# Attention in groups of four query blocks, with the rotary queries of all heads made in the gate-projection stage

## The chip, the cores and the metric

The kernel runs on one core of one Trainium2 chip. The metric is the device time of one execution in microseconds (us), median of three runs. The engines are named as in the profile: PE (TensorE) multiplies matrices, with PEld its weight loads; DVE (VectorE), ACT (ScalarE) and POOL (GpSimd) compute; SP (SyncE) issues most DMAs. L661 is line 661 of the kernel before.

## What is computed

One layer of a streaming encoder, 1024 tokens of width 1024, all in float32: multi-head latent attention with 16 heads, then a gated per-layer embedding. Cut to what matters here:

```python
u = h @ w_in                                  # h = rmsnorm(x)
c_q, c_kv, k_rope, z = split(u)               # 384, 256, 32, 1024 wide
q = rmsnorm(c_q) @ w_q_b                      # 16 heads x (64 + 32 rotary)
kv = rmsnorm(c_kv) @ w_kv_b                   # 16 heads x (64 key + 64 value)
for blk in range(8):                          # blocks of 128 queries
    s = (q_nope . k_nope + q_rope . k_rope) * scale      # keys up to the block's end
    s = where(k_chunk <= q_chunk, s, -inf)               # chunks of 64
    o = softmax(s) @ v
x = x + (o * silu(z)) @ w_out
x = x + sigmoid(rmsnorm(x) @ ple_gate) * (p @ ple_proj)
out = rmsnorm(x, final_norm)
```

Query block i of a head needs the keys of blocks 0 to i, so its scores are 128 x (i+1)*128.

## The kernel before

To hold float32 precision, every operand of a product is split into a high and a low part (`hi`, `lo`, of type fp32r), and a product is the three matmuls hi*hi, hi*lo and lo*hi. Only the product of probabilities with values differs: there the high and low parts of v lie side by side in the 128 columns of one weight tile, and each key block takes two matmuls, one with the high part of the probabilities (`pt..h`) and one with the low part (`pt..l`).

The stages, in order of time:

- **u** (up to 69 us): `u_tile` (L203 to L232) projects eight tiles of 128 tokens to c_q, c_kv and k_rope; `rsqrt` (L93) is three Newton steps on DVE, begun with a shift and a subtraction on the float's bits.
- **z** (69 to 161 us): the loop over c at L503 makes eight blocks of the gate, 48 matmuls of 512 columns each (L513), evicted by DVE (L516) and put through SiLU by ACT. `z_weights` (L347) loads and splits the weights as it goes (L360 on ACT, L361 on DVE). Beside it run `rope_key` (after block 1), `rope_tables` (after block 2: cosine and sine tables by way of DRAM, L446 on DVE, L452 and L485 as DMAs issued by POOL), `weights(0)` (after block 3) and `project_r(0, ...)` (after blocks 4 and 5).
- **attention** (161 to 507 us): 128 blocks (16 heads, 8 query blocks each) in the order `ORDER`. For block n the loop at L685 issues `scores` (L598: matmuls L609, mask L612 and maximum L614 on DVE, exponential L619 on ACT), then work that prepares the next heads, then `prob_transposes` of block n-2 (L641: transposes L121 on PE, high part L650 on ACT, low part L91 on DVE), then `values` for a pair of query blocks that was finished at block n-4 (L653: matmuls L661, addition of the two halves L664 on ACT and L665 on DVE, product with the gate L667 on POOL, on DVE in the last two heads).
- **out, gate and end** (507 us to the end): eight tiles of the output projection, then eight of the gate of the embedding (both L751), the last norm, and the stores to DRAM (L845). `out_part` (L676) prepares the first operand inside the attention's end, and `normalise` (L622) divides by the sums, by way of a small DRAM tile.

What prepares the next heads: `project_k`, `project_q` and `project_v` (L546, L586, L564), and `project_r(g, hf)` (L427), the rotary part of the queries of four heads. It runs 9 matmuls (L423), two DVE multiplications by cosine and sine (L435), a copy on ACT (L438), a subtraction on POOL (L439, recorded as L91) and two DMAs to DRAM on POOL (L441). Group 0 is made during z, groups 1 to 3 in the heads with h%4 == 2 at the block positions `R_AT`. `rope_q(h)` (L578) loads a head's part from DRAM by SP. All of them go through one pair of tiles, `rt` and `rh`.

The tile framework puts each engine's instructions in an order of its own, by priority (the order of the program) and by when it expects them to be ready; at run time each engine then keeps its order and waits on semaphores. PSUM has eight banks of 512 columns: two tiles `big` of two banks each, and four single banks, tag `one`, shared by the transposes, the values and the projections. A block with more than 128 keys has its scores in `big`:

```python
spans = {128: [(0, 256)], 640: [(0, 384), (384, 640)]}.get(
    n, [(a, min(a + 512, n)) for a in range(0, n, 512)])
ps = ps_big() if n > P else ps_tr()
```

The transposed probabilities of a pair of query blocks stand side by side, 256 columns for each key block; where the first block of a pair has no such key block, a block of zeros stands (L539). So the values of pair g are 2(g+1) key blocks times two matmuls of 256 columns.

## Time and profile before

| | us |
|---|---|
| median of 3 runs | 718.59 (717.83 to 719.44) |
| the profiled execution, whole | 719.65 |
| its span in the profile | 717.9 |
| PE busy | 703.2 (98%) |
| DVE, ACT, POOL busy | 523.8, 400.5, 214.2 |
| granted TensorE clock | 0.998 of full speed |

The profile is of one execution. Times in it count from the span's start. A PE matmul is recorded with its passage through the array, so that records overlap: what a matmul costs in a dense row is the distance of the starts, not the recorded length. The chain of waits lists, for a run of instructions without a gap, their number and the time they took together, and from this the cost of one is read.

### The profile page before, as it was taken

To read this page: it belongs to the slowest core of one execution; us is meant where nothing else is said; L and a number is where in the kernel's file an instruction comes from. 1 tells how busy PE (TensorE), PEld (TensorE's weight loads), DVE (VectorE), ACT (ScalarE), POOL (GpSimd) and SP (SyncE) were. 2 spreads that over 40 slices of the span, in tenths; PEclk is the share of its full clock that TensorE was granted. 3 is DMA by queue.
4 is the path that set the end of the run, shared out by engine and by line. 5 is a ranking of instruction groups with operands and counts; after the bars stand their busy time and mean duration, and the time that the engine had idled before them with its cause. 6 is when DMAs were issued, how large, how long until landed. Compare 5 with 4: busy or idle time off the path is not lost.

```text
span 717.9 us, 11582 instructions
## 1 busy us (share of the span) xinstructions
PE 703.2 (98%) x4032; PEld 612.9 (85%) x4032; DVE 523.8 (73%) x1298; ACT 400.5 (56%) x920; POOL 214.2 (30%) x236
## 2 busy tenths in 40 slices
PE   9999999999999999999999999989999999999995
PEld 7999888888988899889988899878878888888884
DVE  6995553417888888888888888899564168888754
ACT  6752343417777767877767787776353145342322
POOL 0000443214145434554335532264155142000000
PEclk9999999999999999999999999999999999999999
DMA  8720334314103402052211421032573030111101
GB/s 318 279 89 12 122 100 125 103 60 110 38 16 108 147 31 74 1 181 74 66 40 60 136 60 60 15 108 85 179 265 115 1 102 24 38 37 37 60 30 59
DMA packets 26907, 63.95 MB, mean 89 GB/s; under 512 B 4568, under 2 KB 8544, under 8 KB 26848
## 3 DMA queue, kind: packets, MB, share of 16 engines
q1 hardware_dynamic: 23168, 52.19, 22.8%
q0 software_dynamic: 3536, 11.02, 4.6%
q8 instruction: 32, 0.52, 0.3%
q14 instruction: 27, 0.22, 0.1%
q10 hardware_dynamic: 144, 0.00, 0.0%
HBM read 50.01 MB, written 13.18 MB: 88 GB/s over the span
## 4 chain that ended last, share of the span: by engine, by line
PE 90%; DVE 3%; ACT 3%; DMA 2%; issue 1%; POOL 0%; SPq 0%; ACTq 0%; DVEq 0%
PE ps_big L751 21%; PE ps_big L609 13%; PE ps_big L513 12%; PE ps_o L661 10%; PE ps_tr L121 9%; PE ps_pj L423 6%; PE ps_big L215 4%; PE ps_pj L751 3%; PE ps_pj L570 3%; PE ps_pj L553 3%; PE ps_big L216 3%; PE ps_o L215 1%; PE ps_pj L216 1%; DMA wst<-in_w_out 1%; ACT prob L619 1%; PE ps_tr L609 1%
## 5 line engine op out<-in xcount | busy, mean ns | idle before, releaser
L751 PE MATMUL ps_big<-w,aTh 128*128 128x512 f32 (+1 forms) x480 | 139.0, 390 | 0.0
L751 PEld LDWEIGHTS ps_big<-w,aTh 128*128 128x128 f32 x480 | 89.4, 188 | 20.2
L619 ACT ACTIVATE prob<-ps_big,mx 128x384 f32<-128x384 f32 (+6 forms) x112 | 89.4, 798 | 16.2 <-DVE mx L614 15.5
L614 DVE TENSOR_REDUCE mx<-ps_big 128x1 f32<-128x384 f32 (+6 forms) x112 | 91.6, 818 | 1.8
L121 PE MATMUL ps_tr<-ident,prob 128*128 128x128 f32 x576 | 84.1, 273 | 2.0 <-ACT prob L619 2.0
L751 PE MATMUL ps_big<-w,aTl 128*128 128x512 f32 (+1 forms) x240 | 84.6, 390 | 0.0
L121 PEld LDWEIGHTS ps_tr<-ident,prob 128*128 128x128 f32 x576 | 68.3, 140 | 11.7 <-ACT prob L619 2.8
L91 DVE TENSOR_TENSOR pt8l<-ps_tr,pt8h 128x512 fp32r<-128x512 f32 (+3 forms) x128 | 71.0, 582 | 4.5 <-ACT pt8h L650 3.8
L667 POOL TENSOR_TENSOR zT<-o,zT 64x256 f32<-64x256 f32 x56 | 41.1, 736 | 94.2 <-DVE o L665 80.6
L609 PE MATMUL ps_big<-k_hi,qh 128*128 128x512 f32 (+2 forms) x176 | 67.7, 385 | 0.9 <-ACT prob L619 0.8
L650 ACT CAST pt8h<-ps_tr 128x512 fp32r<-128x512 f32 (+3 forms) x128 | 60.7, 509 | 4.7 <-PE ps_tr L121 4.3
L609 PE MATMUL ps_big<-k_lo,qh 128*128 128x512 f32 (+2 forms) x176 | 62.0, 352 | 0.0
L609 PE MATMUL ps_big<-k_hi,ql 128*128 128x512 f32 (+2 forms) x176 | 61.4, 349 | 0.0
L661 PE MATMUL ps_o<-pt8h,vals 128*128 128x256 f32 x224 | 57.6, 294 | 0.0
L661 PE MATMUL ps_o<-pt8l,vals 128*128 128x256 f32 x224 | 55.0, 282 | 0.0
L751 PEld LDWEIGHTS ps_big<-w,aTl 128*128 128x128 f32 x240 | 45.0, 188 | 10.2 <-POOL aTl L91 0.5
L116 ACT ACTIVATE jk<-xs 128x512 bf16<-128x512 f32 (+2 forms) x25 | 18.8, 751 | 45.2 <-DVE xs L829 37.3
L661 PEld LDWEIGHTS ps_o<-pt8l,vals 128*128 128x128 f32 x224 | 42.9, 191 | 0.0
L661 PEld LDWEIGHTS ps_o<-pt8h,vals 128*128 128x128 f32 x224 | 42.6, 190 | 0.0
L650 ACT CAST pt4h<-ps_tr 128x384 fp32r<-128x384 f32 (+3 forms) x64 | 27.2, 426 | 27.3 <-PE ps_tr L121 27.1
L360 ACT ACTIVATE zh<-zs,g_col 128x128 fp32r<-128x128 f32 x56 | 18.3, 392 | 42.1 <-DMA zs<-in_w_z 36.1
L609 PEld LDWEIGHTS ps_big<-k_hi,qh 128*128 128x128 f32 x176 | 33.2, 189 | 7.7 <-ACT prob L619 3.5
(285 smaller groups left out, 1740.2 us busy)
## 6 DMA issues: line engine op xcount, KB each, us to landing
...
```

The lines of the kernel that those rows point to most:

```text
L91: eng.tensor_tensor(out=lo, in0=src, in1=hi.bitcast(F32), op=ALU.subtract)
L121: nc.tensor.transpose(dst[:, j * P:(j + 1) * P], src[:, j * P:(j + 1) * P], ident)
L215: nc.tensor.matmul(pq, st, mv[:, k, :QL], start=first, stop=last)
L423: nc.tensor.matmul(ps, w[b][:, k, :], (cq_hi, cq_lo)[a][:, k, hf * 512:hf * 512 + 512], start=k == 0 and a + b == 0, stop=k == n - 1 and a ...
L513: nc.tensor.matmul(ps[:, hf * 512:(hf + 1) * 512], wz[b][:, k % 4, :], (hT_hi, hT_lo)[a][:, k, hf * 512:(hf + 1) * 512], start=k == 0 and ...
L609: nc.tensor.matmul(ps[:, off + s0:off + s1], q[a][:, qs], (k_hi, k_lo)[b][e][:, s0:s1], start=a + b == 0, stop=a == 1)
L614: V.tensor_reduce(out=mx, in_=s, axis=AX.X, op=ALU.max, negate=True)
L619: A.activation(out=pr[:, :n], in_=s, func=AF.Exp, bias=mx, scale=1.0, accum_out=l)
L650: A.copy(out=hi[:, j0:j0 + n, half], in_=src)
L661: nc.tensor.matmul(ps[:, :256], w, z[:, j, :], start=j + n == 0, stop=j == last and n == 1)
L667: (V if h >= H - 2 else G).tensor_tensor(out=z, in0=o[top], in1=z, op=ALU.mult)
L751: nc.tensor.matmul(o, st[a][:, k, :], w[k][b][:, cols], start=k == 0 and a + b == 0, stop=k == nk - 1 and a == 1)
```

## The change

- **Values.** Query blocks stand in two groups of four. For a group, the matmul of a key block covers the query blocks that have it: 512 columns for the key blocks below the group, then 512, 384, 256 and 128 for the four key blocks of the group itself. Each probability tile has as many columns (10 blocks in group 0, 26 in group 1), no zeros are stored, and the evictions (ACT, DVE, POOL) are one of 512 columns a group. The fourth key block of a group of transposes lies apart from the three others, so its copy and subtraction are instructions of their own, twice a head.
- **Order.** Large and small query blocks alternate; `values` is issued ahead of the transposes; projections sit at other positions.
- **Small scores.** Blocks of up to 512 keys take a single bank.
- **Rotary queries.** All four `project_r` are issued in z, one a block from block 2 to 5, through two sets of tiles (two parts of zT not yet written, and `rt`/`rh`). The tables follow block 0 through parts of zT. Their weights are loaded one group ahead (`weights_r`), and `weights(0)` follows block 6.
- **Smaller edits.** `rsqrt` starts with one DVE instruction instead of two and its step uses another form; the staging of odd keys (`kst`) moves to the `rt` tile; the last tile's output goes out in four pieces of 256 columns, one of them by ACT's queue.

```diff
@@ -34,11 +34,11 @@
...
-ORDER = (5, 4, 2, 3, 7, 6, 0, 1)
-LAST = (7, 6, 3, 2, 5, 4, 1, 0)
+ORDER = (7, 0, 6, 1, 5, 2, 4, 3)
+LAST = (7, 0, 6, 1, 5, 2, 3, 4)
...
-V_FIRST = (0, 0, 5, 2)
-V_AT, K_AT, Q_AT, R_AT = (4, 4, 2, 2), (0, 3), (6, 7), (1, 6)
+V_FIRST = (1, 1, 5, 3)
+V_AT, K_AT, Q_AT, ROPE_AT = (5, 5, 3, 3), (1, 3), (7, 5), 4
...
@@ -92,18 +92,15 @@
...
     def rsqrt(v, n, name="rs_y", bufs=None):
...
-        half = small.tile([P, n], I32, tag=f"rs_i{n}", name="rs_i", bufs=2)
-        V.tensor_scalar(out=half, in0=v.bitcast(I32), scalar1=1, scalar2=None,
-                        op0=ALU.logical_shift_right)
...
-        V.tensor_scalar(out=y.bitcast(I32), in0=half, scalar1=-1, scalar2=0x5F3759DF,
+        V.tensor_scalar(out=y.bitcast(I32), in0=v.bitcast(I32), scalar1=-0.5, scalar2=0x5F3759DF,
...
         if n == 1:
...
             for _ in range(3):
-                V.tensor_scalar(out=t, in0=y, scalar1=y, scalar2=h, op0=ALU.mult, op1=ALU.mult)
+                V.scalar_tensor_tensor(out=t, in0=y, scalar=y, in1=h, op0=ALU.mult, op1=ALU.mult)
...
             return y
         for _ in range(3):
@@ -388,27 +385,24 @@
...
-    cs = [att1.tile([P, S], F32, name=f"cs{e}") for e in range(2)]
...
-    def load_split(src, cols, name, bufs):
+    def load_split(src, cols, name, bufs, home=att1):
...
         nc.sync.dma_start(out=stg, in_=src)
-        hi = att1.tile([P, n], F32R, tag=name + "h", name=name + "h", bufs=bufs)
-        lo = att1.tile([P, n], F32R, tag=name + "l", name=name + "l", bufs=bufs)
+        hi = home.tile([P, n], F32R, tag=name + "h", name=name + "h", bufs=bufs)
+        lo = home.tile([P, n], F32R, tag=name + "l", name=name + "l", bufs=bufs)
...
-    wk_of, wv_of, wq_of, wr_of, q_of, rq_of = {}, {}, {}, {}, {}, {}
+    wk_of, wv_of, wq_of, q_of, rq_of = {}, {}, {}, {}, {}
...
     def weights(h):
...
-        if h % 4 == 0:
-            wr_of[h // 4] = load_split(w_r[h // 4], (QL // P, P), "wr", 1)
...
@@ -424,25 +418,23 @@
...
-    def project_r(g, hf):
+    def project_r(g, wr, hf, t, hi):
...
         cols = slice(hf * 512, hf * 512 + 512)
...
-        ps = product_q(wr_of[g], hf)
-        t = rt_tile("rt").rearrange("p (c n) -> p c n", c=2)
+        ps = product_q(wr, hf)
+        t, hi = (z.rearrange("p (c n) -> p c n", c=2) for z in (t, hi))
         for n in range(2):
             V.tensor_tensor(out=t[:, n, :], in0=ps, in1=cs[n][:, cols], op=ALU.mult)
-        hi = rh_tile("rh").rearrange("p (c n) -> p c n", c=2)
         lo = t.bitcast(F32R)
         A.copy(out=hi, in_=t)
         sub_hi(G, lo, t, hi)
...
             nc.gpsimd.dma_start(out=d.rearrange("c p n -> p c n")[:, :, cols], in_=z.bitcast(F32))
...
-    def token_rows(name, src, n):
...
-        blk = rh_tile(name + "b").bitcast(F32)[:, :NT * n]
+    def token_rows(name, src, blk, n):
...
@@ -467,7 +459,7 @@
...
-        d = token_rows("kt", kr, 2 * ROPE)
+        d = token_rows("kt", kr, rh_tile("ktb").bitcast(F32)[:, :512], 2 * ROPE)
...
@@ -476,11 +468,11 @@
...
     def rope_tables():
-        for tab, src, name in zip(cs, (cosT, sinT), ("cos", "sin")):
-            t = rt_tile("spread")[:, :NT * 32].rearrange("p (t n) -> p t n", t=NT)
+        for n, (tab, src, name) in enumerate(zip(cs, (cosT, sinT), ("cos", "sin"))):
+            t, blk = zT[:, 2 + n, :256].rearrange("p (t n) -> p t n", t=NT), zT[:, 2 + n, 256:512]
             V.tensor_copy(out=t.rearrange("p t (m n) -> p t m n", n=HF),
                           in_=src.unsqueeze(2).broadcast_to([P, NT, 32 // HF, HF]))
-            d = token_rows(name, t, ROPE)
+            d = token_rows(name, t, blk, ROPE)
             for i in range(4):
...
@@ -499,6 +491,11 @@
...
+    cs = [zw.tile([P, S], F32, name=f"cs{e}") for e in range(2)]
...
+    def weights_r(g):
+        return load_split(w_r[g], (QL // P, P), "wr", 1, zw)
...
@@ -517,14 +514,18 @@
...
         if c < 2:
             u_transposes(*pend.pop(0))
+        if c == 0:
+            rope_tables()
         if c == 1:
             rope_key()
-        if c == 2:
-            rope_tables()
-        if c == 3:
+            wr = weights_r(0)
+        if 2 <= c < 6:
+            project_r(c - 2, wr, 0, zT[:, 6, :], zT[:, 7, :].bitcast(F32R))
+            project_r(c - 2, wr, 1, rt_tile("rt"), rh_tile("rh"))
+            if c < 5:
+                wr = weights_r(c - 1)
+        if c == 6:
...
-        if c in (4, 5):
-            project_r(0, c - 4)
...
@@ -533,13 +534,9 @@
...
-    pt_w = [[att.tile([P, n, 2 * P], F32R, name=f"pt{n}{z}") for z in "hl"] for n in (4, 8)]
-    for n, w in zip((4, 8), pt_w):
-        for z in w:
-            G.memset(z[:, n - 1, :P].bitcast(F32), 0.0)
-    pt = [[z[:, (2, 0, 2, 0)[g]:, :] for z in pt_w[g // 2]] for g in range(4)]
+    pt = [[att.tile([P, 16 * g + 10, P], F32R, name=f"pt{g}{z}") for z in "hl"] for g in range(2)]
...
-    kst = att.tile([P, S], F32, name="kst")
+    kst = {}
...
@@ -553,13 +550,15 @@
...
-        V.tensor_copy(out=kst[NOPE:, cols], in_=ps[NOPE:])
+        if hf == 0:
+            kst[0] = rt_tile("kst")
+        V.tensor_copy(out=kst[0][NOPE:, cols], in_=ps[NOPE:])
...
-        A.copy(out=k_hi[1][NOPE:], in_=kst[NOPE:])
-        sub_hi(G, k_lo[1][NOPE:], kst[NOPE:], k_hi[1][NOPE:])
+        A.copy(out=k_hi[1][NOPE:], in_=kst[0][NOPE:])
+        sub_hi(G, k_lo[1][NOPE:], kst[0][NOPE:], k_hi[1][NOPE:])
...
@@ -603,7 +602,7 @@
...
-        ps = ps_big() if n > P else ps_tr()
+        ps = ps_big() if n > 512 else ps_tr()
...
@@ -639,31 +638,39 @@
...
     def prob_transposes(h, i, pr):
-        g = i // 2
-        hi, lo = pt[g]
-        half = slice(0, P) if i % 2 == 0 else slice(P, 2 * P)
+        g, q = divmod(i, 4)
         for j0 in range(0, i + 1, 4):
             n = min(4, i + 1 - j0)
             tr = ps_tr()
             transposes(tr, pr[:, j0 * P:(j0 + n) * P], n)
             src = tr[:, :n * P].rearrange("p (k n) -> p k n", n=P)
-            A.copy(out=hi[:, j0:j0 + n, half], in_=src)
-            sub_hi(V, lo[:, j0:j0 + n, half], src, hi[:, j0:j0 + n, half])
+            if j0 < 4 * g:
+                parts = [(slice(0, 4), slice(q, 16, 4))]
+            else:
+                m = min(n, 3)
+                parts = [(slice(0, m), slice(16 * g + q, 16 * g + q + 3 * m - 2, 3))]
+                if n == 4:
+                    parts.append((slice(3, 4), slice(16 * g + 7, 16 * g + 8)))
+            for ks, to in parts:
+                hi, lo = (z[:, to, :] for z in pt[g])
+                A.copy(out=hi, in_=src[:, ks])
+                sub_hi(V, lo, src[:, ks], hi)
...
     def values(h, g):
         e, c = h % 2, h // 2
-        hi, lo = pt[g]
         ps = ps_o()
-        last = 2 * g + 1
-        for j in range(last + 1):
-            w = vals[:, j, c % 2, 2 * e:2 * e + 2, :]
-            for n, z in enumerate((hi, lo)):
-                nc.tensor.matmul(ps[:, :256], w, z[:, j, :], start=j + n == 0, stop=j == last and n == 1)
+        steps = [(j, n) for j in range(4 * g + 4) for n in range(2)]
+        steps.append(steps.pop(1))
+        for j, n in steps:
+            q = max(j - 4 * g, 0)
+            at = 4 * j if j < 4 * g else 16 * g + (7 if q == 3 else 4 * q)
+            nc.tensor.matmul(ps[:, q * P:], vals[:, j, c % 2, 2 * e:2 * e + 2, :],
+                             pt[g][n][:, at:at + 4 - q, :], start=j + n == 0, stop=(j, n) == (0, 1))
         top, bot = slice(e * VD, (e + 1) * VD), slice((1 - e) * VD, (2 - e) * VD)
-        o = att.tile([P, 256], F32, tag="o1", name="o1", bufs=2)
-        A.copy(out=o[top], in_=ps[bot, :256])
-        V.tensor_tensor(out=o[top], in0=ps[top, :256], in1=o[top], op=ALU.add)
-        z = zT[top, c, g * 256:(g + 1) * 256]
+        o = att.tile([P, 512], F32, tag="o1", name="o1", bufs=2)
+        A.copy(out=o[top], in_=ps[bot])
+        V.tensor_tensor(out=o[top], in0=ps[top], in1=o[top], op=ALU.add)
+        z = zT[top, c, g * 512:(g + 1) * 512]
         (V if h >= H - 2 else G).tensor_tensor(out=z, in0=o[top], in1=z, op=ALU.mult)
...
@@ -695,22 +702,21 @@
...
                 if h % 2 and at in K_AT:
                     project_k((h + 1) // 2, K_AT.index(at))
-                if h % 4 == 2 and h + 2 < H and at in R_AT:
-                    project_r(h // 4 + 1, R_AT.index(at))
-                if h % 2 and at == Q_AT[0]:
+                if h % 2 and at == ROPE_AT:
                     rope_q(h + 1)
                     rope_q(h + 2)
                 if h % 2 and at in Q_AT:
                     project_q((h + 1) // 2, Q_AT.index(at))
-                if h % 2 and at == Q_AT[1]:
+                if h % 2 and at == max(Q_AT):
                     weights(h + 3)
+        h, i = blocks[n - LAGV]
+        g = i // 4
+        if n >= LAGV and i == [z for z in order(h) if z // 4 == g][-1]:
+            values(h, g)
+            if h % 2 and i == order(h)[-1] and n < len(blocks):
+                normalise(h // 2, lambda hf: att1.tile([P, 512], F32, tag="ws", name="rlb", bufs=2), G)
         if n >= LAG and n - LAG < len(blocks):
             prob_transposes(*blocks[n - LAG], probs.pop(n - LAG))
-        if n >= LAGV and (blocks[n - LAGV][1] ^ 1) in order(blocks[n - LAGV][0])[:(n - LAGV) % NT]:
-            h, i = blocks[n - LAGV]
-            values(h, i // 2)
-            if h % 2 and i == order(h)[-1] and n < len(blocks):
-                normalise(h // 2, lambda hf: att1.tile([P, 512], F32, tag="ws", name="rlb", bufs=2), G)
...
@@ -835,14 +841,14 @@
...
                 G.tensor_tensor(out=xs[:, t, cols], in0=xs[:, t, cols], in1=f_bc[:, cols], op=ALU.mult)
         r = rsqrt(ms[:, i:i + 1], 1, name="r3", bufs=2)
-        for hf in range(2):
-            cols = halves[hf]
-            if last and hf == 0:
+        for i, cols in enumerate([slice(z, z + 256) for z in range(0, D, 256)] if last else halves):
+            on_act = last and i < 2
+            if on_act:
                 A.activation(out=xs[:, t, cols], in_=xs[:, t, cols], func=AF.Copy, scale=r)
             else:
                 V.scalar_tensor_tensor(out=xs[:, t, cols], in0=xs[:, t, cols], scalar=r,
                                        in1=f_bc[:, cols], op0=ALU.mult, op1=ALU.mult)
-            nc.sync.dma_start(out=out[t * P:(t + 1) * P, cols], in_=xs[:, t, cols])
+            (nc.scalar if on_act and i else nc.sync).dma_start(out=out[t * P:(t + 1) * P, cols], in_=xs[:, t, cols])
...

```

## Rows read from the trace of the kernel before

**Rows 1.** The page: busy time by engine, and the chain of waits by engine

```profile
PE 703.2 (98%) x4032; PEld 612.9 (85%) x4032; DVE 523.8 (73%) x1298; ACT 400.5 (56%) x920; POOL 214.2 (30%) x236
...
PE 90%; DVE 3%; ACT 3%; DMA 2%; issue 1%; POOL 0%; SPq 0%; ACTq 0%; DVEq 0%
```

**Rows 2.** What PE waited for, whole span: total us, times, longest us

```profile
PE ps_tr L121 <- ACT prob L619: 2.0, 2, 1.1
```

**Rows 3.** The chain of waits: start us, us, what, and how many

```profile
269.81 0.87 PE ps_tr L121 x8
...
273.85 1.39 PE ps_pj L553 x6
...
275.35 0.89 PE ps_big L609 x6
276.45 1.92 PE ps_o L661 x16
...
359.51 1.39 PE ps_pj L553 x6
```

**Rows 4.** Timeline of PE's weight loads in head 14: start us, us of one

```profile
470.79 0.19 PEld L609 LDWEIGHTS ps_big<-k_hi,qh 128*128 128x128 f32 x1 [0.49 <-ACT prob L619]
470.90 0.19 PEld L609 LDWEIGHTS ps_big<-k_lo,qh 128*128 128x128 f32 x1
```

**Rows 5.** Windows: stretch, length, each engine's busy us: z, four heads, attention's end

```profile
69.00:161.36 92.36, 92.36 (x413) 76.30 (x412) 39.02 (x103) 32.71 (x79) 29.41 (x42) 1.00 0.34 101
...
273.85:359.51 85.66, 85.66 (x577) 77.68 (x577) 73.53 (x159) 64.47 (x155) 37.80 (x40) 1.00 0.24 74
...
459.21:507.60 48.39, 44.49 (x300) 38.76 (x299) 43.00 (x91) 35.66 (x89) 22.83 (x15) 1.00 0.27 77
```

**Rows 6.** DVE's groups of instructions, 240 to 460 us: busy us, mean ns of one

```profile
L91 DVE TENSOR_TENSOR pt8l<-ps_tr,pt8h 128x512 fp32r<-128x512 f32 x51 | 33.9, 681 | 2.1 <-ACT pt8h L650 2.0
L665 DVE TENSOR_TENSOR o<-ps_o,o 64x256 f32<-64x256 f32 x42 | 17.6, 419 | 3.3 <-ACT o L664 2.7
...
L435 DVE TENSOR_TENSOR rt<-ps_pj,cs 128x512 f32<-128x512 f32 x8 | 5.1, 684 | 1.5 <-PE ps_pj L423 1.5
...
L91 DVE TENSOR_TENSOR pt8l<-ps_tr,pt8h 128x128 fp32r<-128x128 f32 x11 | 3.0, 277 | 0.0
```

**Rows 7.** Timeline of POOL in z: start us, us

```profile
74.01 1.01 POOL L91 TENSOR_TENSOR wrl<-ws,wrh 128x384 fp32r<-128x384 f32 x1
...
103.33 2.33 POOL L452 DMA_DIRECT2D cosd<-cosb  x4 [8.05 <-DVE cosb L446]
...
114.80 1.98 POOL L485 DMA_DIRECT2D cs<-sind  x4 [2.96 <-DMA sind<-sinb]
129.33 2.40 POOL L91 TENSOR_TENSOR rt<-rt,rh 128x1024 fp32r<-128x1024 f32 x1 [12.54 <-ACT rh L438]
...
132.43 0.74 POOL L441 DMA_DIRECT2D rq0l<-rt  x1
```

**Rows 8.** Timeline of DVE, last two heads: the gate product L667, three of eight

```profile
481.03 2.37 DVE L667 TENSOR_TENSOR zT<-o,zT 64x256 f32<-64x256 f32 x1
...
487.19 0.40 DVE L667 TENSOR_TENSOR zT<-o,zT 64x256 f32<-64x256 f32 x1
...
491.46 1.87 DVE L667 TENSOR_TENSOR zT<-o,zT 64x256 f32<-64x256 f32 x1
```

**Rows 9.** Timeline of POOL beside it

```profile
480.75 2.37 POOL L91 TENSOR_TENSOR w<-wst,w 128x1024 fp32r<-128x1024 f32 x1
```

**Rows 10.** Timeline of the last tile's end

```profile
712.53 0.27 DVE L106 TENSOR_SCALAR rs_t<-r,rs_h 128x1 f32<-128x1 f32 x1
712.84 0.16 DVE L107 SCALAR_TENSOR_TENSOR r<-rs_t,r 128x1 f32<-128x1 f32 x1
713.04 0.75 DVE L843 SCALAR_TENSOR_TENSOR xs<-xs,r,f_bc 128x512 f32<-128x512 f32 x1
...
713.84 0.81 SPq L845 DMA_DIRECT2D out<-xs  x2
```

## The prediction

> **What bounds the kernel now.** I read the page first: PE is busy for 98% of the span and holds 90% of the chain that ended last [rows 1]. Then the waits of PE: the longest sum that the view names is 2.0 us in the whole span [rows 2]. So the time is the sum of PE's matmuls, and what each costs has to be read from the distance of starts. The chain gives that: six matmuls of 512 columns in 1.39 us, 0.232 each; sixteen of 256 in 1.92, 0.120 each; eight transposes of 128 columns in 0.87, 0.109 each; and the three pairs 384 + 256 of a 640-key block in 0.89, so 0.297 - 0.120 = 0.177 for 384 [rows 3].
>
> With these prices a head of attention is 6.5 us of scores (three matmuls each of 256, 256, 384, 512, 384 + 256, 512 + 256, 512 + 384 and 512 + 512 columns), 36 transposes (3.9) and 40 values matmuls (4.8), 15.2 us. Four heads with their 24 k, 36 q and 18 rotary matmuls of 512 and 48 v matmuls of 256 come to 85.0 us. The same place in the cycle is reached at 273.85 and at 359.51, 85.66 us apart [rows 3]: PE idles 0.6 us in four heads. Over all of attention (161.36 to 507.60, 346.2 us) my sum is 337.1, so 9.1 us are idle, most of them in the last 48 us, where the heads have no projections left and PE is busy for 44.49 of 48.39 us [rows 5]. The z stage is dense [rows 5].
>
> **The change, part by part.** *Values.* A head had 40 x 0.120 = 4.80 us. It will have 12 matmuls of 512 (2.78), 4 of 384 (0.71), 4 of 256 (0.48) and 4 of 128. The trace has no product of 128 columns, and this price decides the sign. From below: each matmul brings a weight tile of 128 columns, and two loads never start closer than 0.11 us, even after an idle [rows 4]; the transposes, as wide and with as large a load, pay 0.109 [rows 3]. From above: if a narrow product ran its 128 columns four times, it would pay as 512 columns do, 0.232. The transposes are the nearest row, so I take 0.109: 3.97 + 0.44 = 4.41 us a head, -0.39, and **-6.3 us** in 16 heads. At 0.232 it is 4.90, +0.10 a head, +1.6 us. The ends are -6.3 and +1.6.
>
> Here the trace stands against a page. The Trainium skill (TensorE: Matmul & The Clock Gate, section Back-to-back issue gap) gives about 81 ns for a matmul of 128 columns in a stream with weight loads; the transposes here take 109. By its figure the 64 narrow matmuls would cost 1.8 us less, an estimate, and the whole would come out at 710.1.
>
> *Rotary queries.* Three groups of 18 matmuls, 12.5 us, leave attention and enter z at the same price: 0 on PE, as long as z stays dense. What hides the rest there: DVE works 39.0 us of 92.4 in z and POOL 29.4 [rows 5]. DVE gets three times four multiplications of 0.68 [rows 6], 8.2 us; POOL three times two subtractions of 2.40, four DMA issues of 0.74 and a weight split of 1.0 with its copy of about half that [rows 7], 28 us. In a stage that then lasts 105 us that is 47 and 57. The tables, from the first issue at 103.33 to the last at 116.8 [rows 7], took 13.5 us and a landing; moved behind block 0 they have two z blocks of 10.9 us. SP issues the same weight loads as before. `weights(0)` (POOL, about 5 us) goes from block 3 to 6 and has two blocks left. 0, with +5 as the other end if PE has to wait at its first rotary product.
>
> *DVE in attention.* Per four heads it loses four multiplications (2.7 of 73.5 us), gains eight small subtractions (0.28 each, less what the larger ones shed), and saves as much on additions: 16 of 0.42 become 8 of 512 columns, about 0.69 as L435 has it [rows 6]. So 70.8 us beside PE's 85.7 - 4.2 - 1.6 = 79.9: 89% in place of 86% [rows 5]. The heads with h%4 == 2 lose their rotary matmuls, the only filler that they had, while DVE's share of a head stays. I take +0.4 us for each of the four cycles of four heads, **+1.5**, an estimate a little under the 0.6 that a cycle idles now; the ends are 0 and +5.
>
> *Waits added.* The tile of a group is used again by the next head's block 7 while `values` may still read it. The copy on ACT would wait, and the exponentials behind it; but `values` stands ahead of those transposes in PE's queue, so it is over before they are. 0. A group's 16 matmuls are one piece of 3.1 us in which PE hands nothing to DVE; it is part of the +1.5. Small scores: three more blocks a head take a single bank and two fewer `values` do, so 18 takes a head for 17, and `big` is freed. 0.
>
> *Attention's end.* In the last two heads the gate product is DVE's. Two took 2.37 and 1.87 us, another of the same size 0.40 [rows 8]; beside the first POOL was in a subtraction of 2.37 us [rows 9]. There were eight such products, and these two lost 3.4 us; there will be four. Half of that, 1.7, less what the larger last block delays: **-1**, between -4 (half of the idle time there gone) and +2 (the last values are 16 matmuls, 3.1 us, with nothing behind them but the sums).
> The Trainium skill (GPSIMD Engine Reference, section 1. Specifications) says why: GpSimd shares its SBUF interfaces with VectorE, and contends with instructions that have two SBUF inputs. The trace agrees.
>
> *The last tile.* Three steps of 0.27 take the form that costs 0.16 [rows 10], and one short instruction goes: -0.5. The last products, 0.75 each, and the stores [rows 10] become half as large, so the first store leaves about 0.3 earlier and the last is shorter: -0.4, an estimate. **-0.9**, between -1.5 and -0.3. `rsqrt` elsewhere, `kst` and the loads of `rope_q` lie beside PE work: 0; DVE's idle time covers them.
>
> The sum: -6.3 + 0 + 1.5 - 1 - 0.9 = **-6.7 us**. Against the profiled execution (span 717.9, whole 719.65) that is 713.0; the median of the runs, 718.6, lies 1.1 lower, and from it I predict **712.0**.
>
> **The rivals.**
> *1. The narrow matmul costs as much as a wide one.* Nothing in the trace excludes it, and no product here has fewer than 256 columns: blocks of 128 keys are computed 256 wide. Values then give +1.6, the rest -0.4: 719.8, within 717.5 and 721.5.
> *2. POOL becomes late in z; the slower side.* PE takes its products in order, and a rotary product needs the weights that POOL has split. POOL's part of a block is 4.8 + 3.0 + 1.5 = 9.3 us, behind 1.4 of DVE and 1.1 of ACT, 11.8 in all. It decides where this passes the 10.9 us of the z block that follows, with the split last in POOL's order and the halves not overlapped. If PE then waits for one subtraction and its issues, 3.9 us, before each of three groups, 11.7 come on top: 712.0 + 11.7 = 723.7, slower. Against it: the first half starts while PE still works on the second, and POOL stood idle for 12.5 us before its subtraction [rows 7].
> *3. DVE takes the gain back.* If the heads 2, 6 and 10 idle as the last two do, (48.39 - 44.49)/2 = 2 us each [rows 5], and nothing is saved in the last two: -6.3 + 6 + 0.8 - 0.9, 718.2, no change. For it speaks the 89%, against it that DVE's load is now mixed evenly by large and small blocks.
> *4. The end becomes dense too.* Of the 9.1 idle us six go, and DVE costs nothing: -6.3 - 6 - 1.5 = 704.8.
> That the matmuls are not those that the change says cannot be: their number is fixed.
>
> **How the numbers follow.** The forecast 0.58, rival 1 0.20, rival 2 0.07, rival 3 0.07, rival 4 0.08. A measurement of this kernel tells some 0.2%, 1.4 us, from no change, so below 717.2 is faster and above 720.0 slower. Faster: 0.57 of the forecast, 0.03 of rival 1, 0.02 of rival 3 and rival 4, 0.70. Same: 0.10 of rival 1, 0.04 of rival 3, 0.01, 0.15. Slower: rival 2, 0.07 of rival 1, 0.01, 0.15. The forecast's own range is 708 to 716. The range given, 706.5 to 720.0, takes in the upper end of the narrow price and leaves out rival 2, the upper part of rival 1 and the far part of rival 4, about 2 in 10.
>
> **What would show it.** In the chain: values of 512 columns at 0.232, and narrow ones whose successor starts 0.11 later; 0.22 or more is rival 1. Four heads should take some 79.5 us, 82 or more is rival 3. The z stage should last 105 us with no wait of PE for `wrh`, `wrl` or `cs`; 110 or more is rival 2. In the last heads no gate product on DVE over 2 us. The forecast is wrong if attention (first k matmul to last values) shortens by less than 14 us: 12.5 moved and the gain of the values.

## The result, and the profile after: 741.8 us, 3.2% slower

The changed kernel took 741.81 us (median of 4 runs, 740.52 to 742.71) against 718.48 (717.83 to 719.44) of the kernel before: a ratio of 1.0322, 95% interval 1.0302 to 1.0343. The forecast was 712.0 us, its range ended at 720.0. In the profiled execution the span grew from 717.9 to 740.9 us where 711.2 was expected, so 29.7 us have to be found.

The page of the changed kernel: parts 1 and 4, as in [rows 1].

```profile
span 740.9 us, 11048 instructions
...
PE 712.6 (96%) x3776; PEld 599.2 (81%) x3776; DVE 525.6 (71%) x1270; ACT 401.2 (54%) x921; POOL 209.2 (28%) x204
...
PE 69%; DVE 11%; ACT 8%; issue 4%; DMA 3%; POOL 3%; SPq 0%; ACTq 0%; DVEq 0%; POOLq 0%
```

PE's share of the chain fell from 90% to 69%. DVE and ACT, hardly there before, now hold 19% of it. The waits of PE (engine, what waited, releaser: us in total, times, longest) name three that the kernel before did not have, the first, the third and the fourth:

```profile
PE ps_pj L417 <- POOL wrl L91: 4.9, 1, 4.9
PE ps_tr L118 <- ACT prob L618: 3.3, 6, 1.0
PE ps_big L757 <- ACT sg L833: 1.8, 1, 1.8
PE ps_tr L118 <- DVE ps_tr L611: 1.6, 3, 0.6
```

Read by stage, the 29.7 us stand in three places. **z**: from its first product to the first k product it takes 112.3 us where 105.1 was expected, +7.2. **Attention**: from the first k product (181.48) to the start of the last values (526.57) 345.1 us, 346.1 before, where 327.8 was expected, +17.3. By the prediction's prices its matmuls are now 318.3 us, so 26.8 us are idle; before it was 9.1. (The expectations below say 28 and 10: those are sums over the distances of starts.) **Out, gate and end**: 205.9 us from the last values to the last matmul, 201.6 before, +4.3. The start and the last tile hold the remaining 0.9. One part moves between the last two stages: 13 matmuls of the output projection stand ahead of the last values, 5 before. The eight more are 1.9 us of work, so that of attention some 25 us are idle, and out, gate and end lost 6.2 us rather than 4.3.

*z.* The timeline of PE, of the changed kernel:

```profile
148.47 0.40 PE L417 MATMUL ps_pj<-cq_hi,wrh 128*128 128x512 f32 x1
153.79 0.80 PE L417 MATMUL ps_pj<-cq_hi,wrl 128*128 128x512 f32 x1 [4.92 <-POOL wrl L91]
154.38 0.63 PE L417 MATMUL ps_pj<-cq_lo,wrh 128*128 128x512 f32 x1
154.81 0.63 PE L417 MATMUL ps_pj<-cq_hi,wrh 128*128 128x512 f32 x1
```

The second matmul of the fourth rotary group waits for the low part of its weights. Behind the wait the starts are 0.43 us apart, not 0.23. Two stretches show why (columns: stretch, us, busy time of PE, PEld, DVE, ACT, POOL, granted clock, DMA share, GB/s):

```profile
148.40:153.70 5.30, 0.47 (x3) 0.04 (x1) 4.23 (x2) 0.00 (x0) 5.26 (x6) 0.75 0.73 227
153.70:157.70 4.00, 3.91 (x9) 3.15 (x10) 1.26 (x5) 2.22 (x5) 1.26 (x2) 0.50 0.95 363
```

PE stands for 4.9 us; then its first 4.0 us of work run at half the clock (1.2 GHz), which costs 2 us more. What POOL did meanwhile:

```profile
134.80 0.52 POOL L397 CAST wqh<-ws 128x384 fp32r<-128x384 f32 x1
...
140.80 0.40 POOL L397 CAST wkh<-ws 128x256 fp32r<-128x256 f32 x1 [4.39 <-DMA ws<-in_w_k]
...
141.96 0.51 POOL L397 CAST wrh<-ws 128x384 fp32r<-128x384 f32 x1
144.59 0.61 POOL L397 CAST wvh<-ws 128x512 fp32r<-128x512 f32 x1 [2.13 <-DMA ws<-in_w_v]
145.17 2.40 POOL L91 TENSOR_TENSOR zT<-zT 128x1024 fp32r<-128x1024 f32 x1
...
152.73 1.00 POOL L91 TENSOR_TENSOR wrl<-ws,wrh 128x384 fp32r<-128x384 f32 x1
```

The first head pair's wq, wk and wv, written behind all rotary work in the program, stand ahead of the last rotary weight in POOL's order; POOL waits 4.39 us for a load in front of it, and `wrl` comes behind two subtractions and four DMA issues of the group before.

*Attention.* A piece of the chain of waits (start, us, what):

```profile
297.66 3.10 PE ps_o L667 x16
...
306.31 0.59 ACT pt1h L656
...
306.93 0.69 DVE pt1l L91
307.62 0.87 DVE mx L613
...
309.57 0.48 ACT qh L591
...
310.08 0.68 DVE ql L91
```

From 306.3 to 319.6 the chain goes over ACT and DVE alone; before, such a stretch was one row of PE behind the other [rows 3]. This does not mean that PE stands for 13 us: it runs some 70 matmuls meanwhile and loses 0.7 us by the distances of starts. It means that the values at 319.6 could start no earlier than ACT and DVE, handing work to each other, let them. No single wait is long: PE's idle time comes mostly in pieces of 0.2 to 0.6 us, the longest 1.1, and mostly ahead of transposes and of scores in single banks.

### The profile page after: what moved, and what is told of

It reads as the page before. It is cut to its first block, busy times and chain, and to the rows that moved or that the text cites. A ratio compares the mean times of both kernels' runs of the same rounds, so it can differ in the third digit from the quotient of the medians.

```text
span 740.9 us, 11048 instructions
## 1 busy us (share of the span) xinstructions
PE 712.6 (96%) x3776; PEld 599.2 (81%) x3776; DVE 525.6 (71%) x1270; ACT 401.2 (54%) x921; POOL 209.2 (28%) x204
## 4 chain that ended last, share of the span: by engine, by line
PE 69%; DVE 11%; ACT 8%; issue 4%; DMA 3%; POOL 3%; SPq 0%; ACTq 0%; DVEq 0%; POOLq 0%
PE ps_big L757 17%; PE ps_big L510 9%; PE ps_o L667 9%; PE ps_tr L118 6%; PE ps_big L608 5%; PE ps_pj L417 4%; PE ps_big L212 3%; PE ps_pj L569 3%; PE ps_pj L550 3%; ACT prob L618 3%; DVE pt1l L91 3%; PE ps_pj L757 3%; PE ps_big L213 3%; PE ps_tr L608 2%; DVE mx L613 2%
## 5 line engine op out<-in xcount | busy, mean ns | idle before, releaser
L674 POOL TENSOR_TENSOR zT<-o,zT 64x512 f32<-64x512 f32 x28 | 36.0, 1287 | 141.2 <-DVE o L672 141.1
L91 DVE TENSOR_TENSOR pt1l<-ps_tr,pt1h 128x512 fp32r<-128x512 f32 (+1 forms) x144 | 72.7, 536 | 3.9 <-ACT pt1h L656 2.5
L656 ACT CAST pt1h<-ps_tr 128x512 fp32r<-128x512 f32 (+1 forms) x144 | 62.0, 470 | 24.2 <-PE ps_tr L118 12.0
L618 ACT ACTIVATE prob<-ps_big,mx 128x1024 f32<-128x1024 f32 (+1 forms) x64 | 61.3, 958 | 18.3 <-DVE mx L613 17.1
L613 DVE TENSOR_REDUCE mx<-ps_big 128x1 f32<-128x1024 f32 (+1 forms) x64 | 64.9, 1015 | 0.3
L358 DVE SCALAR_TENSOR_TENSOR zl<-zs,g_col,zh 128x128 fp32r<-128x128 f32 x56 | 31.3, 607 | 32.9 <-ACT zh L357 32.6
L667 PE MATMUL ps_o<-pt1h,vals 128*128 128x512 f32 (+3 forms) x128 | 42.9, 361 | 1.5 <-DVE pt1l L91 1.0
L667 PE MATMUL ps_o<-pt1l,vals 128*128 128x512 f32 (+3 forms) x128 | 41.6, 363 | 0.0
L618 ACT ACTIVATE prob<-ps_tr,mx 128x128 f32<-128x128 f32 (+1 forms) x64 | 33.8, 529 | 5.5 <-DVE mx L613 5.3
L91 DVE TENSOR_TENSOR pt0l<-ps_tr,pt0h 128x128 fp32r<-128x128 f32 (+2 forms) x80 | 33.2, 416 | 4.5 <-ACT pt0h L656 2.9
```

What stands on the lines that cost most here:

```text
L91: eng.tensor_tensor(out=lo, in0=src, in1=hi.bitcast(F32), op=ALU.subtract)
L358: V.scalar_tensor_tensor(out=lo[:, k, :], in0=stg[:, k, :], scalar=g, in1=hi[:, k, :].bitcast(F32), op0=ALU.mult, op1=ALU.subtract)
L613: V.tensor_reduce(out=mx, in_=s, axis=AX.X, op=ALU.max, negate=True)
L618: A.activation(out=pr[:, :n], in_=s, func=AF.Exp, bias=mx, scale=1.0, accum_out=l)
L656: A.copy(out=hi, in_=src[:, ks])
L667: nc.tensor.matmul(ps[:, q * P:], vals[:, j, c % 2, 2 * e:2 * e + 2, :], pt[g][n][:, at:at + 4 - q, :], start=j + n == 0, stop=(j, n) == ( ...
```

## The experiments

Attention is given below from the first k product to the last values, and *four heads* from one first k product to the one four heads later, in the middle of attention, where the pattern repeats to 0.1 us: 85.66 before, 84.20 changed. The theories of the expectations have letters. Z: POOL's order in z. R: the new form of the root. In attention, A: ACT's copies wait for DVE's subtractions; B: small scores hold the single banks; C: the order, with C1 for large and small blocks in turn and C2 for the values, 3.1 us in one piece ahead of the transposes; D: DVE, with D1 for its load and D2 for the length of the way from scores to transposes; E: DVE's addition of the halves; F: the rotary matmuls were filler.

**Four edits of the changed kernel.** `z_late`: the call moved behind the loop.

```diff
-        if c == 6:
-            weights(0)
+    weights(0)
     zph.close()
```

> Edit: in the changed kernel the first head pair's weights are loaded and split behind the z loop, not at c == 6, so GpSimd has nothing but the rotary work in its queue. Theory Z (the casts and splits of wq, wk and wv stand in GpSimd's order ahead of the last rotary group's low part, and TensorE waits in order for that): TensorE's 4.9 us wait for wrl and the ten matmuls at half clock go, z to the last z product goes from 112.2 to 105 us, the time from 741.8 to about 734.5 us. Rival (GpSimd's eight subtractions of 2.4 us and sixteen DMA issues are too much by themselves): a wait for wrl of 3 us or more stays, z 110 us or more, the time over 739 us.

740.84 us, 1.0295 (1.0269 to 1.0320). This did not yet test the theories: POOL's order stayed the same (wq at 133.48, `wrl` at 152.72), and so did the wait, 4.8 us. Here the framework did not place the loads by where the call stands.

`rsqrt_old`:

```diff
-                V.scalar_tensor_tensor(out=t, in0=y, scalar=y, in1=h, op0=ALU.mult, op1=ALU.mult)
+                V.tensor_scalar(out=t, in0=y, scalar1=y, scalar2=h, op0=ALU.mult, op1=ALU.mult)
```

> Edit: in the changed kernel the one-column reciprocal root takes its product by tensor_scalar again (two operands from scalar pointers) instead of scalar_tensor_tensor. Theory R (the new form reads two tensors from SBUF and is held up by a GpSimd subtraction, 2.3 us each: two of them were hit around 614 to 619 us, VectorE was 2.3 us later at the last output tile's sum, the first sigmoid and TensorE with it): the 1.9 us wait at the gate's start and the half-clock matmuls behind it go, the gate's start is 3 us shorter, the time 741.8 to about 738.5 us, with 0.2 us given back in the last tile. Rival (the wait comes from the last gate weight, which landed 2 us later than before): the wait stays over 1.3 us, the time within 1 us of 741.8.

740.46 us, 1.0302 (1.0271 to 1.0332); the wait was still 1.3 us, though without half the clock behind it. The new form alone is not the cause, so theory R falls. In the changed kernel's timeline of DVE, and POOL beside it:

```profile
614.25 2.26 DVE L104 SCALAR_TENSOR_TENSOR r<-rs_t,r 128x1 f32<-128x1 f32 x1
616.54 2.31 DVE L103 SCALAR_TENSOR_TENSOR rs_t<-r,rs_h 128x1 f32<-128x1 f32 x1
...
614.09 4.74 POOL L91 TENSOR_TENSOR w<-wst,w 128x1024 fp32r<-128x1024 f32 x2 [5.93 <-ACT w L742]
```

and in `rsqrt_old`, where both hits fall on L104, the step that the edit leaves as it was:

```profile
617.39 2.15 DVE L104 SCALAR_TENSOR_TENSOR r<-rs_t,r 128x1 f32<-128x1 f32 x1
...
619.88 1.99 DVE L104 SCALAR_TENSOR_TENSOR r<-rs_t,r 128x1 f32<-128x1 f32 x1
...
617.13 4.74 POOL L91 TENSOR_TENSOR w<-wst,w 128x1024 fp32r<-128x1024 f32 x2 [5.85 <-ACT w L742]
```

One column takes 0.16 to 0.22 us, and 2.0 to 2.3 while POOL subtracts. In `z_late`, with the new form, one was hit (2.32 us) and PE did not wait there. In the changed kernel the chain of waits goes over both hits to PE's wait, and ahead of them back to the load of the last gate weight (602.11 to 608.36), so the rival in the expectation is not excluded. The wait at the gate's start looks like chance of position, which a shift of the stages ahead can bring; no run tests that by itself.

`copies_first`:

```diff
             for ks, to in parts:
                 A.copy(out=pt[g][0][:, to, :], in_=src[:, ks])
+            for ks, to in parts:
                 sub_hi(V, pt[g][1][:, to, :], src[:, ks], pt[g][0][:, to, :])
```

> Edit: in the changed kernel, where a block's four transposes go out in two pieces, both high copies (ScalarE) are written ahead of both low subtractions (VectorE). Theory A (the first piece's slots stand three apart and enclose the second's; the second copy is made to wait for the first piece's subtraction although they share no element, ScalarE stands 15 us in attention for it and the exponentials queue behind): that wait falls under 2 us, attention from the last z product to the last values goes from 345.3 to 335 us or less, the time to about 731 us. Theory B (small scores hold a single bank until their exponential) and theory C (values in lumps of 3.1 us ahead of the transposes, blocks in turn): attention stays within 3 us of 345.3, the time over 738 us.

741.97 us, 1.0299 (1.0269 to 1.0328), attention 345.7. The wait went and another took its place. ACT's waits from 184 to 500 us, first of the changed kernel, then of `copies_first`:

```profile
ACT pt1h L656 <- DVE pt1l L91: 9.7, 11, 1.0
ACT o L671 <- PE ps_o L667: 9.3, 21, 0.9
```

```profile
ACT o L671 <- PE ps_o L667: 25.2, 22, 2.3
```

Theory A falls. `big_scores`:

```diff
-        ps = ps_big() if n > 512 else ps_tr()
+        ps = ps_big() if n > P else ps_tr()
```

> Edit: in the changed kernel all scores of more than one key block go to the double-bank tiles again, so that only the smallest block's scores take a single bank. Theory B (the four small scores of a head hold a single bank each until their exponential, and transposes, values and projections wait for a bank): attention goes from 345.3 to 335 us or less, the time to about 731 us. Theories A and C: attention within 3 us of 345.3, or longer, since the two double-bank tiles now turn over seven times a head rather than four; the time 739 to 746 us.

742.33 us, 1.0322 (1.0293 to 1.0352), attention 349.4, four heads 85.29. Theory B falls: the single banks are worth 4.3 us as they are. Without them PE waits for a double bank, 9.4 us from 184 to 500 us:

```profile
PE ps_big L608 <- ACT prob L618: 9.4, 10, 1.4
```

**The z stage settled.** `z_after` makes the loads depend on the rotary work:

```diff
+            t, u = rt_tile("ws0"), rh_tile("ws1").bitcast(F32)
+            own = [u[:, :QL], t[:, :KVL], t[:, 512:]]
```

> Edit: in the changed kernel the first head pair's weights (wq, wk, wv) are staged in the two tiles of the odd rotary halves instead of the two staging tiles that the rotary weights use, so that they can't be loaded before the last rotary group has left; moving the call alone had left them where they were in GpSimd's order. Theory Z (these three loads and splits hold up the last rotary group's low part): the 4.9 us wait for wrl goes, z goes from 112.2 to 105 us, the time to about 734.5 us; if the first key projection has to wait for wk, up to 3 us of it come back at attention's start. Rival (GpSimd is late by its subtractions and DMA issues alone): a wait for wrl of 3 us or more stays, z 110 us or more.

732.87 us, 1.0178 (1.0160 to 1.0196), 8.9 less than the changed kernel. z takes 105.3 us, and PE waits nowhere in it, with all of POOL's rotary work still there; POOL's timeline has the last rotary weight split in time:

```profile
138.56 1.02 POOL L91 TENSOR_TENSOR wrl<-ws,wrh 128x384 fp32r<-128x384 f32 x1
```

The whole of z in `z_after`, as a stretch (columns as above):

```profile
69.40:174.60 105.20, 105.20 (x468) 86.66 (x467) 60.97 (x110) 39.31 (x86) 50.66 (x56) 1.00 0.45 152
```

Theory Z holds; 7.0 of z's 7.2 us were this. The gate's wait was gone as well, without an edit to it.

**The parts of attention one at a time.** `pairs_rz` is the kernel before with `project_r` in z:

```diff
+            project_r(c - 2, wr, 0, zT[:, 6, :], zT[:, 7, :].bitcast(F32R))
+            project_r(c - 2, wr, 1, rt_tile("rt"), rh_tile("rh"))
...
-                if h % 4 == 2 and h + 2 < H and at in R_AT:
-                    project_r(h // 4 + 1, R_AT.index(at))
```

> Edit: the kernel before, with the rotary queries made during z as in the changed kernel, and nothing else of the change: values in pairs of query blocks, the old order, double-bank scores, the old root and last tile. Theory F (the rotary products were what TensorE did in attention while ScalarE and VectorE caught up; without them it stands): attention, from the last z product to the last values, stays over 341 us of the 346.1 before, the time over 732 us. Theories C and D (grouping and order, or VectorE's load under the shorter values, make the idle time): attention shortens by the rotary products' 12.5 us to 333 to 336 us, z is 112 us as in the changed kernel, and the time is 724 to 728 us.

732.66 us, 1.0184 (1.0157 to 1.0211). Attention 338.3: between the two. 12.5 us of matmuls left and 7.8 us came back. Where the rest stays can be read from single heads. Head 6, from its first scores to those of the next head, before and in `pairs_rz` (columns as above):

```profile
294.82:313.54 18.72, 18.72 (x126) 16.79 (x124) 15.91 (x35) 13.92 (x35) 10.01 (x11) 1.00 0.26 85
```

```profile
313.51:331.11 17.60, 16.37 (x115) 14.63 (x114) 15.60 (x35) 13.87 (x37) 7.79 (x9) 1.00 0.17 54
```

By the distances of starts the heads 2, 6 and 10, where the rotary queries were made, now idle 2.3 us each, 0.2 before; the other heads idle no more than before. So it was the filler that was lost, with DVE at 15.60 of 17.60 us in such a head.

`pairs_alt` adds the order to it (and the places of the projections):

```diff
-ORDER = (5, 4, 2, 3, 7, 6, 0, 1)
+ORDER = (7, 0, 6, 1, 5, 2, 4, 3)
```

> Edit: pairs_rz (the kernel before with the rotary queries in z) with the changed kernel's order of blocks, positions of the projections, and values ahead of the transposes; values stay in pairs, scores in double banks. Theory C1 (taking large and small blocks in turn costs idle time by itself): attention from 338.3 to 346 us or more, the time from 732.7 to 740 us. Theory D2 with groups of four (the lumps of values and the split copies lengthen the way): attention within 4 us of 338.3, the time within 4 us of 732.7.

739.13 us, 1.0272 (1.0253 to 1.0292), attention 344.4: +6.1, with values still in pairs: between the marks of C1 (346) and of D2 (342.3), nearer to C1. Order, places and values ahead were changed together here. `old_order` goes the other way, groups of four with the large blocks first:

```diff
-ORDER = (7, 0, 6, 1, 5, 2, 4, 3)
+ORDER = (5, 4, 7, 6, 2, 3, 0, 1)
```

> Edit: in the changed kernel the blocks of a head are taken large ones first, small ones behind (5, 4, 7, 6, 2, 3, 0, 1) with the positions of the projections of before, instead of large and small in turn; groups of four, single banks and rotary queries in z stay. Theory C1 (taking large and small blocks in turn makes the idle time): attention from 345.3 to 335 us or less, the time to about 731 us. Theories C2 (lumps of values), D (VectorE's load) and F: attention 342 us or more, the time 739 us or more; under D it can be worse, since the large blocks' maxima and subtractions then come in one row.

769.95 us, 1.0690 (1.0669 to 1.0711), attention 378.3. With groups of four the alternation is not what costs: with this order they lose 33 us more. `values_after` puts values behind the transposes again (the second group's then read a tile in which the next head's first block already stands).

> Edit: in the changed kernel a group's values are asked for behind the transposes of the same step again, as before. Theory C2 (3.1 us of values ahead of the transposes hold ScalarE and VectorE back): attention falls from 345.3 to 338 us or less, the time to about 734 us. Theory D (VectorE): attention within 4 us of 345.3; it is longer if the high copies of the next head then have to wait for these values, which read the same tile.

767.47 us, 1.0655 (1.0629 to 1.0681), attention 372.4: C2 falls, values belong ahead of the transposes.

**Load or way.** `light_dve`:

```diff
-        V.tensor_reduce(out=mx, in_=s, axis=AX.X, op=ALU.max, negate=True)
+        V.tensor_reduce(out=mx, in_=ident, axis=AX.X, op=ALU.max, negate=True)
```

> Edit: in the changed kernel the row maximum is taken over a constant 128x128 tile instead of the block's scores, and the exponential gets a scale of 0.001, so the probabilities are others; the matmuls, transposes, copies and subtractions stay. It takes some 4 us per head off VectorE (maxima of 0.28 to 1.21 us become about 0.25 us each), and shortens the way from scores to exponential. Theory D (VectorE, 85% busy in every head, and in order, is what TensorE's 28 us of idle time in attention go back to): attention falls to 327 us or less, the time under 724 us. Theories C and F (order, lumps or missing filler, with the waits on ScalarE or on the banks): attention stays over 338 us.

724.90 us, 1.0067 (1.0041 to 1.0092), attention 329.7: 15.4 us less, 2.7 short of D's mark. `half_lo`:

```diff
-                sub_hi(V, lo, src[:, ks], hi)
+                sub_hi(V, lo[:, :, :64], src[:, ks, :64], hi[:, :, :64])
```

> Edit: in the changed kernel the subtraction that makes the low part of the transposed probabilities takes 64 of each 128 queries, the low part of the others is set to zero once; everything else stays. It takes some 3 us per head off VectorE, as light_dve took 4 us, but off the way from the probabilities to the values, and leaves the way from scores to exponential as it is. Theory D1 (VectorE's load: whatever it is spared shortens the queue in front of everything it does): attention falls from 345.3 to 335 us or less. Theory D2 (the length of the way from scores over maximum and exponential to the transposes, which light_dve also cut by up to 1 us a block): attention stays over 341 us.

732.10 us, 1.0173 (1.0152 to 1.0193), attention 339.4, between the marks of D1 and D2. Four heads in stretches, of the changed kernel, of `light_dve` and of `half_lo` (columns as above):

```profile
295.56:379.76 84.20, 82.74 (x494) 70.54 (x494) 69.71 (x155) 62.31 (x153) 27.37 (x24) 1.00 0.17 50
```

```profile
289.35:370.97 81.62, 81.43 (x497) 70.14 (x495) 57.28 (x154) 61.16 (x153) 27.36 (x24) 1.00 0.18 51
```

```profile
293.79:377.24 83.45, 82.59 (x495) 70.19 (x494) 60.29 (x155) 62.15 (x153) 27.39 (x24) 1.00 0.18 50
```

DVE lost 12.4 and 9.4 us in four heads, PE won 2.6 and 0.75: not in proportion. The maxima weigh more, perhaps since they also stand on the way to the exponential. Two runs were to part the load from the way, and neither did. `max_aside` gives the exponential a constant bias and leaves the maximum to DVE, read by nobody:

```diff
-        A.activation(out=pr[:, :n], in_=s, func=AF.Exp, bias=mx, scale=1.0, accum_out=l)
+        A.activation(out=pr[:, :n], in_=s, func=AF.Exp, bias=one, scale=1e-3, accum_out=l)
```

> Edit: in the changed kernel the exponential takes a constant bias (and a scale of 0.001, so the probabilities are others) and no longer waits for the row maximum; VectorE still takes every maximum over the block's scores, and nobody reads it. VectorE's load is that of the changed kernel; the way from scores to exponential is shorter by 0.3 to 1.2 us a block. Theory D2 (the length of the way): attention falls from 345.3 to 333 us or less, near light_dve's 329.7. Theory D1 (VectorE's load and queue): attention stays over 340 us, and half_lo's 5.9 us and light_dve's 15.6 us are what 3 and 4 us per head are worth.

738.30 us, 1.0260 (1.0224 to 1.0296), attention 346.4. Its timeline of DVE and ACT:

```profile
346.11 0.11 DVE L613 MEMSET ps_big<- 64x64 f32 x1
...
346.91 0.95 DVE L615 TENSOR_REDUCE mx<-ps_big 128x1 f32<-128x768 f32 x1
...
347.96 0.90 ACT L620 ACTIVATE prob<-ps_big,one 128x768 f32<-128x768 f32 x1 [1.30 <-DVE mx L615]
```

The exponential still starts 0.1 us behind the maximum's end, though it takes nothing from it, and in none of the 128 blocks does it start ahead of that end. Both read one tile of PSUM, which is the likely reason; no run shows it. The way was not shortened. `max_behind` takes the maximum from the probabilities instead:

```diff
+        V.tensor_reduce(out=mx, in_=pr[:, :n], axis=AX.X, op=ALU.max, negate=True)
```

> Edit: in the changed kernel the exponential takes a constant bias (and a scale of 0.001, so the probabilities are others), and VectorE takes a maximum of the same length behind it, over the probabilities, that nobody reads. The maximum can't start ahead of the exponential now, and nothing on the way from scores to transposes waits for it; VectorE's load stays within 2 us per four heads of the changed kernel's 69.7. Theory D2 (the length of the way): attention falls from 345.3 to 334 us or less, near light_dve's 329.7. Theory D1 (VectorE's load): attention stays over 340 us.

740.76 us, 1.0289 (1.0268 to 1.0310), attention 348.9, four heads 86.41. By the expectation that is D1; but DVE now stood in its own order for the exponentials, 24.8 us from 184 to 500 us, so the run is no clean test:

```profile
DVE mx L620 <- ACT prob L618: 24.8, 55, 1.2
```

**More room for the way**, on `z_after`. `z_prob4` has two probability tiles of 1024 columns and two of 512; `z_lag3` and `z_lag3b` also move transposes and values back by a block (in `z_lag3` a head's second group of values can meet the v of the next four heads).

```diff
-LAG, LAGV, LEAD, ODD_AT = 2, 4, 2, 1
+LAG, LAGV, LEAD, ODD_AT = 3, 5, 2, 1
```

> Edit: z_after with four probability tiles in two sizes (two of 1024 columns, two of 512) in place of three of 1024; order and distances stay. Theories D1 and D2: attention within 2 us of 345.2, the time 731 to 735 us, since an exponential rarely waits for a probability tile. Rival (the exponential of a block waits until the transposes of the block three before have left its tile): attention shorter by 5 us or more.

> Edit: z_after with a block's transposes asked for three blocks behind its scores instead of two, values five instead of four, and four probability tiles (two of 1024 columns, two of 512) in place of three. Theory D2 (the way from scores to transposes is too long for two blocks, with VectorE's load as it is): attention falls from 345.2 to 335 us or less, the time from 732.9 to about 722 us. Theory D1 (VectorE's load): attention stays within 4 us of 345.2, since the same work passes through VectorE in the same order; the time 729 to 737 us.

> Edit: z_after with transposes three blocks behind the scores, values five, and four probability tiles in two sizes, as z_lag3, but with the projection of the next four heads' v placed so that no value has to pass it (z_lag3 had the second group's values behind it, which made that run's result another and its waits longer). Theory D2: attention from 345.2 to 337 us or less, the time from 732.9 to about 724 us. Theory D1: attention within 4 us of 345.2, or longer, since high copies of the next head come later behind values that read the same tile.

`z_prob4` 733.36 us, 1.0197 (1.0175 to 1.0218), attention 345.0: the tiles were not it. `z_lag3` 752.02, 1.0449 (1.0434 to 1.0465), and `z_lag3b` 757.60, 1.0523 (1.0500 to 1.0547), attention 368.0: later is worse. D2 falls as these two runs put it; D1 had allowed a longer time for `z_lag3b`, but for `z_lag3` 737 us at most.

**The addition of the halves.** `z_o_pool`, on `z_after`:

```diff
-        V.tensor_tensor(out=o[top], in0=ps[top], in1=o[top], op=ALU.add)
+        A.copy(out=u[top], in_=ps[top])
+        G.tensor_tensor(out=o[top], in0=u[top], in1=o[top], op=ALU.add)
```

> Edit: z_after, with the two halves of a group's values both copied by ScalarE and added by GpSimd, in place of one copy by ScalarE and an addition by VectorE. VectorE loses two instructions of 0.69 us per head and its 21 us of waiting for them in order; ScalarE gets two of 0.58 us per head more, GpSimd two of 1.3 us. Theory E (VectorE stands in its order at this addition until the lump of values is through, and everything behind it is late): attention falls from 345.2 to 338 us or less, the time from 732.9 to about 725 us. Rival (load for load: what VectorE gives up ScalarE takes, and the exponentials wait there instead): attention 343 us or more, the time 731 us or more.

747.84 us, 1.0394 (1.0370 to 1.0418), attention 359.3, +14.1 on `z_after`. The gain of theory E did not come. Four heads:

```profile
289.55:376.91 87.36, 82.84 (x494) 70.83 (x494) 64.59 (x147) 66.56 (x161) 37.45 (x32) 1.00 0.17 48
```

DVE is lighter by 5 us than in the changed kernel, ACT heavier by 4, and four heads take 3.2 longer. So less load on DVE does not help whatever else is done. But this run does not price ACT's load either: the edit also leaves the tiles of the halves one buffer each, where `o` had two, and ACT, from 184 to 500 us, waits until POOL's product has left it:

```profile
ACT o L676 <- POOL zT L680: 9.1, 4, 3.6
```

**The end alone.** `tail_alone` is the kernel before with the changed last tile and root.

```diff
-        for hf in range(2):
+        for i, cols in enumerate([slice(z, z + 256) for z in range(0, D, 256)] if last else halves):
```

> Edit: the kernel before, with the changed kernel's last tile (four pieces of 256 columns, two scaled by ScalarE, one store from ScalarE's queue) and its reciprocal root, and nothing else of the change. The forecast's last term was 0.9 us off the end; the changed kernel's trace shows 8.5 us from the last matmul's start to the end where before it was 8.9 us. By the trace: 718.2 us, 0.4 us less than before, hardly to be told from no change; by the forecast's term 717.7 us. Rival (the root's new form is held up by GpSimd's subtractions at the gate's start, as two of its instructions were in the changed kernel): slower by 1 to 3 us.

718.40 us (12 runs) against 719.34 (17 runs), 0.9990 (0.9978 to 1.0002): not told from no change. No version tried is shown to beat the kernel before.

## Why the prediction was wrong, point by point

*Values: right.* The first narrow matmul, its successor with the wide one behind it, and the transposes that follow, in PE's timeline:

```profile
300.14 0.23 PE L667 MATMUL ps_o<-pt1h,vals 128*128 128x128 f32 x1
300.20 0.56 PE L667 MATMUL ps_o<-pt1l,vals 128*128 128x128 f32 x2
300.60 0.60 PE L118 MATMUL ps_tr<-ident,prob 128*128 128x128 f32 x4
```

The first successor comes 0.06 us later, but the three take 0.46 together; less 0.23 for the wide one that is 0.115 each. I took 0.109, so rival 1 falls. (One support was too strong: some 40 of the 4031 pairs of successive weight loads in the trace before do start closer than 0.11 us, 0.06 to 0.10 apart.) The Trainium skill's 81 ns for 128 columns (TensorE: Matmul & The Clock Gate, section Back-to-back issue gap) is not what these rows show.

*Rotary queries in z: right for the products, wrong on POOL.* "`weights(0)` (POOL, about 5 us) goes from block 3 to 6 and has two blocks left" is the sentence that failed: it takes the place in the program for the place in POOL's order. The end "+5 as the other end if PE has to wait at its first rotary product" had the kind, not the product nor the half clock behind it. Rival 2 (0.07) had the wait, PE for weights that POOL splits late, in one group instead of three: 7.2 us where it gave 11.7. Its reason was another: it had POOL late by the rotary work itself, and in `z_after` POOL does all of that work and PE waits nowhere. z is 105.3 us there; my 105 was right.

*Attention: the step that failed.* The terms *DVE in attention*, +1.5, and *Waits added*, 0, stand where 17.3 us went. The ladder of the runs, with what I had expected of each rung:

| kernel | attention | step | expected | four heads |
|---|---|---|---|---|
| before | 346.1 | | | 85.66 |
| `pairs_rz`: rotary out | 338.3 | -7.8 | -12.5 | 83.48 |
| `pairs_alt`: order, values ahead | 344.4 | +6.1 | 0 | 84.30 |
| `big_scores`: groups of four | 349.4 | +5.0 | -6.3 | 85.29 |
| changed: single banks | 345.1 | -4.3 | 0 | 84.20 |

The shortfalls are 4.7, 6.1 and 11.3 us, less 4.3: 17.8 in all, and 17.3 with the terms +1.5 and -1. (`big_scores` also has the changed tail and a moved `kst`; and of the output's matmuls 5, 5, 12, 8 and 13 stand in attention down the table, at 0.23 us each.) So the single banks, which I put at nothing, helped attention, and the grouping, the change's point, cost more than its matmuls saved. That holds with double banks: pairs of query blocks with single banks were not run.

Four heads say which term was mis-sized. 85.66 less the 4.2 us of rotary matmuls is 81.5, and `pairs_rz` takes 83.48: the filler taken out costs 2.0 us a cycle, where the prediction had 0.4 for it and for all else in DVE's way. With the values' 1.6 us off as well it would be 81.9, and 84.20 came: 2.3 us more for order, grouping and single banks together, which the prediction put into the same 0.4 or at 0. (The mark of 79.5 us was a slip besides: the prediction's own terms give 79.9, and 80.3 with the 0.4.)

Rival 3 (0.07) had the first of the two, place and price: it said 2 us in each of the heads 2, 6 and 10, and in `pairs_rz` they idle 2.3. In the changed kernel its mark, 82 us or more for four heads, is passed, but there PE idles some 16 us more than before, not 6, and in every head, 0.4 to 2.6 us by the distances of starts.

Why a part of the matmuls' gain does not arrive, the runs show only in outline. Taking 12.4 us off DVE in every four heads, some 50 in all, and shortening the way with it (`light_dve`) gives back 15.4 us of attention; PE then idles some 11 us in it, nearly as little as the 9 before. ACT and DVE hand each block to and fro in fixed orders, busy for 74 and 83% of the time, and where the rotary matmuls are gone PE has less to lay between. A share of 89% or 86% that I compared could not show this: the changed kernel's DVE is at 83% and PE idles. Whether the load or the length of the way decides is open, as is what the grouping itself does to the orders.

*Attention's end.* The four gate products on DVE took 0.67 to 0.69 us, none over 2, as said; whether that gave the 1 us is lost in the rest.

*The last tile: mis-sized.* From the last matmul's start to the end it is 8.48 us against 8.82, -0.3 for -0.9. The new form takes 0.23 in the chain, not 0.16, for 0.28 before. The root gives all of the 0.3; the four smaller pieces, from the first product's start to the end, take 4.8 us as the two larger did, so their -0.4 did not come. For `rsqrt` elsewhere, put at 0, the two hits at the gate's start stand against it in the profiled execution; `tail_alone`, which has the same root, is not slower.

*Out and gate* were not in the sum: +4.3. The wait of 1.8 us at the gate's start, with the clock at half for 3.4 us behind it, is 3 of it:

```profile
628.87:632.28 3.41, 3.41 (x10) 2.67 (x9) 1.99 (x6) 0.72 (x2) 0.00 (x0) 0.50 0.13 41
```

The other runs have 200 to 204 us there with nearly the same code; why is open.
